# Hybrid decoder layer: a head pair's key-query products issued as one bunch, the second half into another PSUM tag

## The chip, the cores and the metric

The kernel runs on one NeuronCore of a Trainium2 chip. The metric is the device time of one execution in microseconds (us). Five engines take part: TensorE (PE, matmuls; its weight loads are shown apart as PEld), VectorE (DVE), ScalarE (ACT), GpSimd (POOL) and the DMA queues, most of which SyncE (SP) feeds. Results of matmuls land in PSUM, which has eight banks of 128 x 512 float32; DVE and ACT read them out.

## The reference

One decoder layer over 512 tokens of width 1024. Its first half normalises x, projects it, feeds two mixers (an RWKV-7 recurrence of 16 heads of 64 and a sparse attention), merges them by gates and projects back; its second half is a gated MLP with a short causal convolution. The change touches the recurrence only:

```python
def step(state, inp):                       # for each of the 512 tokens, each of the 16 heads
    r_t, w_t, k_t, v_t, a_t, b_t = inp
    sa = jnp.einsum('bhvk,bhk->bhv', state, a_t)
    state = (state * w_t[:, :, None, :] + sa[..., None] * b_t[:, :, None, :]
             + v_t[..., None] * k_t[:, :, None, :])
    return state, jnp.einsum('bhvk,bhk->bhv', state, r_t)
```

## The kernel before

The recurrence isn't run token by token. The 512 tokens are cut into 8 chunks of 64. Inside a chunk everything is matrix products; between chunks a state of 64 x 64 per head is carried on. Heads are worked in pairs p = 0 to 7, one head on partitions 0 to 63 and the other on 64 to 127, and the pairs in two groups of four (g = 0 and 1).

What a pair goes through:

- `inputs(p)` projects the normalised x to K, R and V, three blocks of 8 x 3 matmuls of 128x512 each (lines 297, 298, 299: weight-high times x-high, weight-high times x-low, weight-low times x-high). These are long, and they are what PE does while other work is being prepared.
- `decay(p)` and `prep(p)` make the decay factors and scaled operands. `decay` multiplies `pw` (lines 516, 517) and `pa` (523, 524) into PSUM; ACT turns them into T and A, POOL and DVE go on to EC and EN. `prep` ends with the operands KB (keys and the b vectors, scaled) and AR (a and r, scaled). Line 579 on POOL is the last write of KB.
- `couple(p)` forms, for each chunk c and head h, the 128x128 product of KB and AR: the key-query products, tile `g`, line 607. Chunks 0 to 3 are the half q = 0 and chunks 4 to 7 the half q = 1; a half fills two banks, `g{p}{q}0` and `g{p}{q}1`, one for each head. DVE multiplies each bank with the causal mask into the tile GS in SBUF (line 610) and so frees it. After both halves POOL scales KB for the state (line 617, which overwrites KB and so has to wait until the products have read it), V is transposed into `pv`, a correction is multiplied into `pbo` (626, 627), and the local products `pl` (636) and the transposes `pt` of KB are made.

After a group's four pairs, `invert` inverts the small triangular systems on DVE, and `recur` walks over the 8 chunks (tiles xw, xs, y; `YT` on ACT, line 739, reads `y` out). `stats` and `finish` normalise the result (tiles `gst`, `YT`; lines 787 to 799). They run among the pairs of the second group.

PSUM is shared by four tags of two banks each: `pj` for the projections, `px`, `py` and `pz`. Before the change both halves of `g` use `pz`, as do `pw`, `pa` and `pbo`. `py` holds `pl`, one of the two `pt`, and in the recurrence `y`.

Generators interleave these pieces: `drive` steps the projection of the next pair and, at given rates, `couple`, `decay` and `prep`. Each `yield` is a step. Tile's scheduler then sets each engine's final order by its own list scheduling from that program order, the dependencies and the buffers, so that an edit in `couple` can move instructions of other pieces, on every engine. In the profile a float32 matmul counts twice (x16 for the 8 products of a half), and each product has a weight load of its own, on 64 rows of the array where the projections use 128.

Of the kernel before, what the change touches and what calls it, by code (L numbers as in the profile page):

```python
# [48 lines left out]
def hybrid_layer(ctx: ExitStack, tc: tile.TileContext, a, out, dbg=None, stop=None):  # L49
# [14 lines left out]
    def pj(name):  # L64
        return ps.tile([128, 512], F32, tag="pj", name=name, bufs=2)

    def px(name):
        return ps.tile([128, 512], F32, tag="px", name=name, bufs=2)

    def py(name):  # L70
        return ps.tile([128, 512], F32, tag="py", name=name, bufs=2)

    def pz(name):
        return ps.tile([128, 512], F32, tag="pz", name=name, bufs=2)
# [44 lines left out]
    def tr(o, i, ident):  # L119
        return te.transpose(o, i, ident)  # L120
# [467 lines left out]
    def decayed(p, o, gr):  # L588
        po.tensor_tensor(gr.AR[p % GP][:, 1, :].rearrange(c8, t=64), o.R.rearrange(c8, t=64), o.EC[:, :, 1:65],
                         op=OP.mult)  # L590
        sc.activation(gr.Dc[:, p % GP], o.EC[:, :, 64], AF.Copy)

    def couple(p, o, gr, i):
        V, EC, KB = o.V, o.EC, o.KB
        AR = gr.AR[i]
        if i == 0:
            sc.activation(AR[:, 0, :], o.AR, AF.Copy)
            decayed(p, o, gr)
            yield
        m4 = mask.rearrange("p (s t) -> p s t", t=64)[:, None].to_broadcast([128, 4, 2, 64])  # L600
        for q in range(2):
            gh = [pz(f"g{p}{q}{h}") for h in range(2)]
            for j in range(4):
                c = 4 * q + j
                for h in range(2):
                    hs = slice(h * 64, (h + 1) * 64)
                    te.matmul(gh[h][:, j * 128:(j + 1) * 128], KB[hs, c].rearrange("p s t -> p (s t)"),  # L607
                              AR[hs, :, c * 64:(c + 1) * 64], start=True, stop=True)
            for h in range(2):
                ve.tensor_tensor(gr.GS[:, 0:2 + i:1 + i, 4 * q:4 * q + 4, h].rearrange("p s c t -> p c s t"),  # L610
                                 gh[h].rearrange("p (c s t) -> p c s t", s=2, t=64), m4, op=OP.mult)
            yield
        for b in range(2):
            bs = slice(b * 32, (b + 1) * 32)
            sy.dma_start(gr.ld[b, i].rearrange("c h i t -> i (c h) t"), gr.GS[bs, 0, :, :, bs])
        sy.dma_start(gr.l2[i].rearrange("c h i t -> i (c h) t"), gr.GS[0:32, 0, :, :, 32:64])
        po.tensor_tensor(KB.rearrange("p c s t -> p c (s t)"), KB.rearrange("p c s t -> p c (s t)"),  # L617
                         EC[:, :, 64:65].to_broadcast([128, 8, 128]), op=OP.mult)
        pv = px(f"pv{p}")
        for t in range(4):  # L620
            tr(pv[:, t * 128:t * 128 + 128], V[:, t * 128:t * 128 + 128], ident)
        for q in range(2):
            sc.activation(gr.UV[64:128, q::2, i], pv[64 * q:64 * q + 64].rearrange("p (c h f) -> p c h f", h=2, f=64),
                          AF.Copy)
        pbo = pz(f"pbo{p}")
        te.matmul(pbo, onesr, o.rbh, start=True, stop=False)
        te.matmul(pbo, onesr, o.rbl, start=False, stop=True)
        bv = rw.tile([128, S], F32, tag="T", name=f"bv{p}", bufs=NT)
        ve.tensor_tensor(bv, pbo, V, op=OP.mult)
        yield  # L630
        yield
        sy.dma_start(bvd[p], bv)
        pl = py(f"pl{p}")
        for c in range(8):
            for h in range(2):
                te.matmul(pl[h * 64:(h + 1) * 64, c * 64:(c + 1) * 64], gr.GS[64:128, 0, c, h, :],
                          gr.UV[64:128, c, i, h, :], start=True, stop=True)
        pt = [f(f"pt{p}{q}") for q, f in enumerate((py, px))]
        for c in range(8):
            tr(pt[c // 4][:, c % 4 * 128:c % 4 * 128 + 128], KB[:, c].rearrange("p s t -> p (s t)"), ident)  # L640
        sc.activation(gr.LV[:, i], pl.rearrange(c8, t=64), AF.Copy)
        for q in range(2):
            sc.activation(gr.BKT[i][:, 4 * q:4 * q + 4, :], pt[q].rearrange("p (c f) -> p c f", f=128), AF.Copy)
        yield
# [220 lines left out]
    for g in range(2):  # L865
        group_tiles(g)
        for i in range(GP):
            p = GP * g + i
            if i < GP - 1:
                drive(inputs(p + 1, os_[p + 1]), spawn(couple(p, os_[p], G[g], i), 0, PR),  # L870
                      spawn(later(decay, p + 1, os_[p + 1], pz), 4, 0.5),
                      spawn(later(prep, p + 1, os_[p + 1], pz, G[g]), KD, PK))
            else:
                drive(itertools.chain(*gates_(1)), spawn(couple(p, os_[p], G[g], i), 0, PL))
        if g == 0:
            r0 = core(0)
            fill = itertools.chain(*gates_(NG0), inputs(GP, os_[GP]))
            drive(fill, *r0, spawn(later(decay, GP, os_[GP], pz), 8 * NG0 + 4, 0.5),
                  spawn(later(prep, GP, os_[GP], pz), 8 * (NG0 + 3) + 1, PA))
            f0 = spawn(finish(G[0], 0), 0, FR)  # L880
# [493 lines left out]
    with pool("ff") as ff:  # L1374
# [29 lines left out]
        for j in range(22):  # L1404
            us = []
            for x in range(2):
                blk = 2 * j + x
                if blk < NU:
                    p = pu4[blk]
                    half_up(blk, 1)  # L1410
                else:
                    wh, wl = split_w(a["up"][blk], f"up{blk}")
                    p = pj(f"pu{blk}")
# [242 lines left out]
```

## Time and profile before

| | |
|---|---|
| median of 3 runs | 1181.39 us (1176.57, 1181.39, 1184.37) |
| the profiled execution's own time | 1176.54 us |
| its span | 1174.8 us |
| PE busy, PE weight loads busy | 1144.2 us (97%), 914.0 us (78%) |
| DVE, ACT, POOL busy | 685.8, 604.4, 560.1 us |
| mean granted TensorE clock | 0.992 |
| pairs 0 to 3, products of `g` | 93 to 169 us |
| pairs 4 to 7, products of `g` | 294 to 379 us |

A profile is of one execution, so what is read from it is compared with that execution's time, 1176.54 us, not with the median. In rows of the chain and of the timeline the first number is the start, the second the duration, in us from the span's start. "[0.56 <-DVE GS L610]" at a row's end means that the engine was idle for 0.56 us before it, and that DVE's instruction of line 610 on tile GS ended the wait.

### The profile page before, as it was taken

The page shows a single profiled execution, that of the slowest core. Times are in us where ns is not written, and L with a number is a line of the kernel's source. Part 1 is how long each engine was busy: PE and PEld are TensorE (multiplying, and loading weights), DVE is VectorE, ACT ScalarE, POOL GpSimd, SP SyncE. Part 2 cuts the span into 40 slices and gives each one's busy share as a digit, 9 for nine tenths or more (in the row PEclk, how much of TensorE's full clock was granted, in tenths as well). Part 3 has the DMA queues.
Part 4 walks back from the last instruction along what each step waited for, and adds up shares of the span by engine and source line. Part 5 has one row for each costly group of instructions (what it writes and reads, how often), then busy time and mean ns, then how long its engine had stood idle before and what let it go on. Part 6 is the DMA issues. An engine that isn't in the chain of part 4 may idle for free.

```text
span 1174.8 us, 19913 instructions
## 1 busy us (share of the span) xinstructions
PE 1144.2 (97%) x7316; PEld 914.0 (78%) x7316; DVE 685.8 (58%) x1350; ACT 604.4 (51%) x1208; POOL 560.1 (48%) x535
## 2 busy tenths in 40 slices
PE   8999999999899999999999999999999999999997
PEld 6887788877687888766766777788888888887886
DVE  4245547344655652577699985655443544548776
ACT  5546554433565433476576664443344444446664
POOL 4356765544777553455433212531266666664300
PEclk9999999989999999999999999999999999999999
DMA  6522334530134556236342125551155555559941
GB/s 215 138 74 83 103 111 143 182 89 25 54 105 123 178 161 164 86 99 212 108 126 82 37 64 169 198 200 38 56 143 150 143 146 144 145 152 208 200 112 71
DMA packets 115250, 147.93 MB, mean 126 GB/s; under 512 B 47249, under 2 KB 50129, under 8 KB 114898
## 3 DMA queue, kind: packets, MB, share of 16 engines
q1 hardware_dynamic: 93890, 121.76, 34.1%
q0 software_dynamic: 6336, 11.54, 5.9%
q10 hardware_dynamic: 14928, 13.37, 3.4%
q8 instruction: 57, 0.93, 0.3%
q14 instruction: 39, 0.32, 0.1%
HBM read 124.29 MB, written 21.23 MB: 124 GB/s over the span
## 4 chain that ended last, share of the span: by engine, by line
PE 81%; DVE 7%; issue 5%; POOL 4%; ACT 2%; DMA 1%; SPq 0%; DVEq 0%; POOLq 0%; ACTq 0%
PE pu L193 6%; PE pu L192 6%; PE pu L194 6%; PE da L1465 5%; PE pt L120 3%; PE o L1118 3%; PE db L1465 3%; PE gt L297 2%; PE gt L299 2%; PE gt L298 2%; PE ub L1147 2%; PE ub L1145 2%; PE g L607 2%; PE ub L1146 2%; PE v L297 1%
## 5 line engine op out<-in xcount | busy, mean ns | idle before, releaser
L1420 DVE SCALAR_TENSOR_TENSOR u<-pu,cvec,u 128x511 f32<-128x511 f32 x44 | 32.9, 748 | 98.7 <-ACT u L1419 98.7
L1426 POOL TENSOR_TENSOR ar<-u,u 128x512 f32<-128x512 f32 x22 | 28.7, 1303 | 38.7 <-DVE u L1421 38.7
L658 DVE TENSOR_TENSOR TM<-XL 128x30 f32<-128x30 f32 (+14 forms) x60 | 32.1, 536 | 20.7 <-ACT XL L653 18.7
L1391 ACT ACTIVATE oh<-ar 128x512 fp32r<-128x512 f32 (+1 forms) x44 | 25.1, 573 | 33.9 <-DVE ar L1428 26.6
L1118 PE MATMUL o<-PT,vt 128*64 128x128 f32 (+3 forms) x256 | 40.4, 441 | 0.0
L660 DVE TENSOR_TENSOR XL<-XL,TM 128x30 f32<-128x30 f32 (+14 forms) x60 | 35.7, 596 | 2.2
L1104 ACT ACTIVATE PT<-pt 128x384 f32<-128x384 f32 (+1 forms) x48 | 24.8, 517 | 23.1 <-PE pt L120 22.9
L1419 ACT ACTIVATE u<-pu,cvec 128x512 f32<-128x512 f32 x44 | 33.5, 762 | 5.2 <-PE pu L1355 5.2
L1106 DVE COPY PT<-pt 128x384 f32<-128x384 f32 (+1 forms) x48 | 28.6, 596 | 11.2 <-PE pt L120 10.8
L1421 DVE SCALAR_TENSOR_TENSOR u<-pu,cvec,u 128x510 f32<-128x510 f32 x44 | 32.9, 749 | 1.5
L1392 DVE TENSOR_TENSOR ol<-ar,oh 128x512 fp32r<-128x512 f32 (+1 forms) x44 | 27.1, 620 | 9.0 <-ACT oh L1391 8.8
L521 DVE TENSOR_TENSOR_SCAN C<-rmask,T 128x512 f32<-128x512 f32 x8 | 10.8, 1356 | 36.1 <-POOL T L520 36.0
L610 DVE TENSOR_TENSOR GS<-g,mask 128x512 f32<-128x512 f32 x32 | 20.7, 685 | 14.3 <-PE g L607 14.3
L1118 PEld LDWEIGHTS o<-PT,vt 128*64 128x64 f32 x256 | 15.6, 136 | 14.9 <-issue 11.7
L607 PEld LDWEIGHTS g<-AR,KB 64*128 64x128 f32 x256 | 18.9, 192 | 8.9 <-DVE GS L610 3.9
L607 PE MATMUL g<-AR,KB 64*128 64x128 f32 x256 | 22.3, 291 | 2.9 <-POOL KB L579 1.4
L1428 DVE TENSOR_TENSOR ar<-ar 128x256 f32<-128x256 f32 x11 | 15.4, 1398 | 15.8 <-POOL ar L1426 15.8
L1423 ACT ACTIVATE u<-u 128x512 f32<-128x512 f32 x22 | 13.7, 624 | 18.8 <-DVE u L1421 18.7
L977 POOL TENSOR_SCALAR rh<-dist 128x512 f32<-128x512 f32 x16 | 10.3, 643 | 26.0 <-DVE stt L1023 13.2
L766 ACT ACTIVATE UV<-xs 64x256 f32<-64x256 f32 x16 | 6.1, 379 | 31.6 <-PE xs L671 23.2
L617 POOL TENSOR_TENSOR KB<-KB,EC 128x1024 f32<-128x1024 f32 x8 | 15.3, 1917 | 11.5 <-PE g L607 6.2
L1321 PE MATMUL wo<-woh,mh 128*128 128x512 f32 x52 | 20.4, 392 | 0.0
(2710 smaller groups left out, 4324.6 us busy)
## 6 DMA issues: line engine op xcount, KB each, us to landing
wt<-in_down_dram POOLq DMA_DIRECT2D x33, 256.0 KB, 5.0
gtd<-gt ACTq DMA_DIRECT2D x16, 256.0 KB, 2.0
qs<-qd SPq DMA_DIRECT2D x32, 128.0 KB, 2.9
g<-gtd SPq DMA_DIRECT2D x16, 256.0 KB, 3.4
wt<-in_down_dram SPq DMA_DIRECT2D x11, 256.0 KB, 3.2
w<-in_down_dram SPq DMA_DIRECT2D x11, 256.0 KB, 3.3
w<-in_down_dram POOLq DMA_DIRECT2D x11, 256.0 KB, 4.7
dna<-in_down_dram SPq DMA_DIRECT2D x11, 256.0 KB, 4.7
```

The costliest lines, as they stand in the source:

```text
L120: return te.transpose(o, i, ident)
L192: te.matmul(p, wh(k), mh(k), start=first and k == 0, stop=False)
L193: te.matmul(p, wh(k), ml(k), start=False, stop=False)
L194: te.matmul(p, wl(k), mh(k), start=False, stop=last and k == n - 1)
L297: te.matmul(p, wh(k), hh[:, k, :], start=k == 0, stop=False)
L607: te.matmul(gh[h][:, j * 128:(j + 1) * 128], KB[hs, c].rearrange("p s t -> p (s t)"), AR[hs, :, c * 64:(c + 1) * 64], start=True, stop=True)
L660: ve.tensor_tensor(XU[:, j + 1:32, 0:j], XU[:, j + 1:32, 0:j], tm, op=OP.add)
L1118: te.matmul(po8[e * 64:e * 64 + 64, j * 128:], vt[:, j, b * 256 + g * 64:b * 256 + g * 64 + 64], PT[j, e], start=False, stop=b == 1 and j ...
L1419: sc.activation(u, p, AF.Identity, scale=cvec[:, cv + 2:cv + 3], bias=cvec[:, cv + 3:cv + 4])
L1420: ve.scalar_tensor_tensor(u[:, 1:], p[:, :S - 1], cvec[:, cv + 1:cv + 2], u[:, 1:], op0=OP.mult, op1=OP.add)
L1421: ve.scalar_tensor_tensor(u[:, 2:], p[:, :S - 2], cvec[:, cv:cv + 1], u[:, 2:], op0=OP.mult, op1=OP.add)
L1465: te.matmul(acc[m], l[k][:, x, tsl], w[r], start=first and i == 0, stop=last and i == 2, skip_group_check=True)
```

## The change

Both halves' products are issued one after the other as one bunch of 16, ahead of either half's masking. The first half still takes `pz`, the second takes `py`.

```diff
@@ couple
+        gq = []
         for q in range(2):
-            gh = [pz(f"g{p}{q}{h}") for h in range(2)]
+            gh = [(pz, py)[q](f"g{p}{q}{h}") for h in range(2)]
             for j in range(4):
                 c = 4 * q + j
                 for h in range(2):
                     hs = slice(h * 64, (h + 1) * 64)
                     te.matmul(gh[h][:, j * 128:(j + 1) * 128], KB[hs, c].rearrange("p s t -> p (s t)"),
                               AR[hs, :, c * 64:(c + 1) * 64], start=True, stop=True)
+            gq.append(gh)
+        for q, gh in enumerate(gq):
             for h in range(2):
                 ve.tensor_tensor(gr.GS[:, 0:2 + i:1 + i, 4 * q:4 * q + 4, h].rearrange("p s c t -> p c s t"),
                                  gh[h].rearrange("p (c s t) -> p c s t", s=2, t=64), m4, op=OP.mult)
             yield
```

The lines behind it stand three further down (607 becomes 608, 610 becomes 613, 617 becomes 620). The number of instructions stays the same. On TensorE the scheduler moves other rows at two of the eight pairs, 0 and 4; at the others the products alone move. On ScalarE rows move at the same two pairs, on GpSimd at 0, 4 and 6, on VectorE at 4, and on SP some loads and stores change places near pairs 4 and 6.

TensorE at pair 0, from the end of the first half on, before (the digits of `g` are pair, half, head; `k1` is the next pair's projection, `pv0` a transpose of V):

```order
L607 MATMUL g000_963<-AR00_916,KB0_857 128x128
L607 MATMUL g001_964<-AR00_916,KB0_857 128x128
L298 MATMUL k1_938<-hl_110,w7h1_945 128x512
L299 MATMUL k1_938<-hh_109,w7l1_946 128x512
L297 MATMUL k1_938<-hh_109,w7h1_945 128x512
L607 MATMUL g010_981<-AR00_916,KB0_857 128x128 x3
L607 MATMUL g011_982<-AR00_916,KB0_857 128x128 x3
L607 MATMUL g010_981<-AR00_916,KB0_857 128x128
L607 MATMUL g011_982<-AR00_916,KB0_857 128x128
L298 MATMUL k1_938<-hl_110,w7h1_945 128x512
L299 MATMUL k1_938<-hh_109,w7l1_946 128x512
L120 MATMUL pv0_1016<-ident_81,V0_824 128x128 x2
```

The same place now:

```order
L608 MATMUL g010_973<-AR00_916,KB0_857 128x128
L608 MATMUL g011_974<-AR00_916,KB0_857 128x128
L298 MATMUL k1_938<-hl_110,w7h1_945 128x512
L299 MATMUL k1_938<-hh_109,w7l1_946 128x512
L516 MATMUL pw1_993<-ltw_398,lh1_931 128x512
L517 MATMUL pw1_993<-ltw_398,ll1_932 128x512
L523 MATMUL pa1_1001<-lta_399,lh1_931 128x512
L524 MATMUL pa1_1001<-lta_399,ll1_932 128x512
```

The eight products of the second half follow the first half's eight directly (these rows begin with the last two of them), and `pw` and `pa` of the next pair come ahead of `pv0`. At pairs 1, 2, 3, 5, 6 and 7 the bunch closes in the same way, and the three to seven rows that stood between the halves now stand behind it.

TensorE at pair 4, where the first group's recurrence ends, before (from behind the first half on; `r5` is the next pair's projection, `pt40` and `pt41` the transposes of KB):

```order
L120 MATMUL pv4_3111<-ident_81,V4_2539 128x128 x4
L299 MATMUL r5_3132<-hh_109,w18l0_3134 128x512
L297 MATMUL r5_3132<-hh_109,w18h1_3139 128x512
L298 MATMUL r5_3132<-hl_110,w18h1_3139 128x512
L607 MATMUL g410_3073<-AR10_3004,KB4_2661 128x128 x4
L607 MATMUL g411_3074<-AR10_3004,KB4_2661 128x128 x4
L636 MATMUL pl4_3161<-UV1_3013,GS1_3008 64x64 x2
L516 MATMUL pw5_3085<-ltw_398,lh5_3019 128x512
L517 MATMUL pw5_3085<-ltw_398,ll5_3020 128x512
L636 MATMUL pl4_3161<-UV1_3013,GS1_3008 64x64 x7
L120 MATMUL pt40_3178<-ident_81,KB4_2661 128x128 x3
L523 MATMUL pa5_3093<-lta_399,lh5_3019 128x512
```

The same place now, from the last two products on:

```order
L608 MATMUL g410_3065<-AR10_3004,KB4_2661 128x128
L608 MATMUL g411_3066<-AR10_3004,KB4_2661 128x128
L516 MATMUL pw5_3085<-ltw_398,lh5_3019 128x512
L517 MATMUL pw5_3085<-ltw_398,ll5_3020 128x512
L523 MATMUL pa5_3093<-lta_399,lh5_3019 128x512
L524 MATMUL pa5_3093<-lta_399,ll5_3020 128x512
L120 MATMUL pv4_3111<-ident_81,V4_2539 128x128 x4
L120 MATMUL pt41_3179<-ident_81,KB4_2661 128x128 x4
L299 MATMUL r5_3132<-hh_109,w18l0_3134 128x512
L297 MATMUL r5_3132<-hh_109,w18h1_3139 128x512
L298 MATMUL r5_3132<-hl_110,w18h1_3139 128x512
L299 MATMUL r5_3132<-hh_109,w18l1_3140 128x512
```

Here `pw5`, `pa5`, `pv4` and half of the transposes of KB moved to just behind the bunch, ahead of the projection rows that stood between the halves, and the local products `pl4` moved behind those.

GpSimd at the same place, before (`w20l1` is a weight's low part for V of pair 5, `YT0` the recurrence's output, `T5` and `F5` are decay factors of pair 5):

```order
L508 MEMSET TT1_3015 32x32x32 x2
L140 TENSOR_TENSOR w20l1_3244<-w201r_3245,w20h1_3243 128x512
L789 TENSOR_TENSOR YT0_2528<-YT0_2528,gst01_3051 128x512
L617 TENSOR_TENSOR KB4_2661<-KB4_2661,EC4_2354 128x1024
L534 MEMSET EC6_3452 128x8
L789 TENSOR_TENSOR YT0_2528<-YT0_2528,gst01_3051 128x512
L520 TENSOR_SCALAR T5_3089<-T5_3089 128x512
L528 TENSOR_SCALAR F5_3098<-A5_3096,vd_94 128x512
```

And now:

```order
L508 MEMSET TT1_3015 32x32x32 x2
L792 TENSOR_TENSOR YT0_2528<-YT0_2528,gst01_3051 128x512
L620 TENSOR_TENSOR KB4_2661<-KB4_2661,EC4_2354 128x1024
L534 MEMSET EC6_3452 128x8
L140 TENSOR_TENSOR w20l1_3244<-w201r_3245,w20h1_3243 128x512
L520 TENSOR_SCALAR T5_3089<-T5_3089 128x512
L792 TENSOR_TENSOR YT0_2528<-YT0_2528,gst01_3051 128x512
L528 TENSOR_SCALAR F5_3098<-A5_3096,vd_94 128x512
```

The weight's low part moved behind the scaling of KB, and the second `YT0` behind `T5`. On VectorE the four maskings of pair 4 stand closer together, the third and fourth ahead of two reductions of `stats`.

## The prediction

> **What bounds the kernel now.** I read the page first, its busy shares and its costliest groups. The columns of a group are the count, busy us and mean ns of one, and behind the second bar the engine's idle time just before them with what ended most of it.
>
> ```profile
> PE 1144.2 (97%) x7316; PEld 914.0 (78%) x7316; DVE 685.8 (58%) x1350; ACT 604.4 (51%) x1208; POOL 560.1 (48%) x535
> ...
> L610 DVE TENSOR_TENSOR GS<-g,mask 128x512 f32<-128x512 f32 x32 | 20.7, 685 | 14.3 <-PE g L607 14.3
> ...
> L607 PEld LDWEIGHTS g<-AR,KB 64*128 64x128 f32 x256 | 18.9, 192 | 8.9 <-DVE GS L610 3.9
> L607 PE MATMUL g<-AR,KB 64*128 64x128 f32 x256 | 22.3, 291 | 2.9 <-POOL KB L579 1.4
> ```
>
> TensorE is the bound: busy for 97% of the span, so only what shortens its own stream, or a wait in it, moves the end. The products of `g` are 22.3 us of that stream, about 1.9%. They had 8.9 us of idle weight loading ahead of them, of which 3.9 us were ended by the maskings of line 610. The change can't remove any of the 22.3 us. It can remove waits for a masking, and whatever it costs TensorE to turn from the projections to the products and back twice instead of once. So the stake is a few us of 1176.5, and the question is how many.
>
> The second view is the chain of waits around a pair where nothing waits, pair 1, from its second half on (start, duration, what):
>
> ```profile
> 118.48 1.09 PE g L607 x16
> 119.57 0.43 PE k L297
> 120.00 0.23 PE k L298
> ```
>
> A projection matmul takes 0.23 us here, but the first one behind a half takes 0.43 us. Each half so costs 1.09 us plus 0.20 us of turning. How long eight more products last inside a running bunch I take from their weight loads at pair 7, with which they are paced:
>
> ```profile
> 374.50 0.97 PEld L607 LDWEIGHTS g<-AR,KB 64*128 64x128 f32 x16 [0.35 <-POOL w60l L140]
> ```
>
> 16 loads in 0.97 us. A second half that follows the first directly should thus add 0.97 us, and the projection that stood behind it falls back to 0.23 us.
>
> **The change, pair by pair.** It adds and removes no instruction. At each pair I set what the second half and the projection behind it take now against 0.97 + 0.23 = 1.20 us.
>
> *Pairs 1, 2 and 6, where no masking is waited for.* Pair 1 is above; the second halves of pairs 2 and 6 are
>
> ```profile
> 143.14 1.09 PE g L607 x16
> 350.41 1.09 PE g L607 x16
> ```
>
> so each has 1.09 + 0.43 = 1.52 us and saves 0.32 us: **0.96 us** for the three. Bounds for one pair: 0.20 us, if the bunch runs no tighter than two halves, and 0.55 us, the whole of 0.12 + 0.43. I take 0.32, since both its parts are rows.
>
> *Pairs 0 and 3, where the second half is stretched.* Both halves want the two banks of `pz`, and with only three projection rows between them the masking hasn't freed the second bank when the first is refilled:
>
> ```profile
> 95.06 1.64 PE g L607 x16
> 96.70 0.43 PE k L298
> ...
> 166.93 1.63 PE g L607 x15
> 168.56 0.43 PE gt L297
> ```
>
> 1.64 + 0.43 and 1.63 + 0.43 become 1.20 each: 0.87 and 0.86, together **1.73 us**. The second half has banks of its own in `py`, whose last users there, `pl` and `pt` of the pair before, were read out long ago. At pair 0 `pw` and `pa` now come two projections behind the bunch and want the `pz` banks; the maskings start as the first half ends, take 0.69 us each and run beside the second half's 0.97 us, so I cost that at nothing.
>
> *Pair 7, the longest wait.* Here DVE comes late to the maskings, so the second half first waits and is then stretched. The first row is of the timeline, the second of the chain:
>
> ```profile
> 377.34 1.75 PE L607 MATMUL g<-AR,KB 64*128 64x128 f32 x16 [0.79 <-DVE GS L610]
> 379.10 0.43 PE gt L297
> ```
>
> 0.79 + 1.75 + 0.43 = 2.97 us become 1.20: **1.77 us**, the largest term. What is late next is the masking itself, which no longer holds up TensorE, since the local products that read GS stand well behind it in its order.
>
> *Pair 5, at a lowered clock.* The first row is of the timeline, the next of the chain; the last is of the view by stretches, which has columns of busy us per engine, then the granted clock, the DMA share and GB/s:
>
> ```profile
> 317.99 0.50 PE L299 MATMUL k<-hh,w22l 128*128 128x512 f32 x1 [2.75 <-POOL w22l L140]
> 322.23 0.43 PE k L298
> ...
> 323.08 1.51 PE g L607 x16
> 324.59 0.43 PE k L297
> 319.00:325.00 6.00, 5.79 (x40) 4.48 (x41) 1.67 (x3) 0.63 (x1) 3.92 (x6) 0.72 0.54 167
> ```
>
> TensorE waits 2.75 us for a weight's low part from POOL, and then runs at a mean clock of 0.72: a projection takes 0.43 us, the second half 1.51. The saving lies between the 0.32 of a quiet pair and 1.51 + 0.43 - 0.97 - 0.43 = 0.54, if the bunch runs before the clock falls. I take **0.4 us**.
>
> *Pair 4, where the order changes.* This is the one place where a masking wait may only change its name (the timeline, engine by engine):
>
> ```profile
> 295.19 1.08 ACT L739 ACTIVATE YT<-y 128x512 f32<-128x512 f32 x2 [0.85 <-PE y L671]
> 297.29 1.26 POOL L140 TENSOR_TENSOR w20l<-w201r,w20h 128x512 fp32r<-128x512 f32 x1 [1.31 <-PE r L299]
> 297.64 0.96 PEld L607 LDWEIGHTS g<-AR,KB 64*128 64x128 f32 x8 [0.56 <-DVE GS L610]
> 298.50 0.68 DVE L610 TENSOR_TENSOR GS<-g,mask 128x512 f32<-128x512 f32 x1
> 298.73 1.04 POOL L789 TENSOR_TENSOR YT<-YT,gst 128x512 f32<-128x512 f32 x1 [0.17 <-DVE gst L788]
> 299.23 0.96 PEld L607 LDWEIGHTS g<-AR,KB 64*128 64x128 f32 x8 [0.62 <-DVE GS L610]
> 300.47 1.91 POOL L617 TENSOR_TENSOR KB<-KB,EC 128x1024 f32<-128x1024 f32 x1 [0.70 <-PE g L607]
> 301.75 0.69 ACT L519 ACTIVATE T<-pw,vd 128x512 f32<-128x512 f32 x1
> 302.44 0.55 PE L120 MATMUL pt<-ident,KB 128*128 128x128 f32 x3 [0.52 <-POOL KB L617]
> 304.98 0.48 PE L299 MATMUL r<-hh,w18l 128*128 128x512 f32 x1
> ```
>
> Two waits of 0.56 and 0.62 us for maskings go. New ones come. The second half takes the `py` banks, which hold the recurrence's last `y` until ACT has read it at 296.27, about when the first half ends: some 0.1 us. `pa` wants the bank that the second masking frees at 299.2. And four transposes of KB now stand ahead of four projections and wait for line 617 on POOL; that is behind `YT`, ends no sooner than 298.73 + 1.04 + 1.91 = 301.7, and finds TensorE ready at about 300.1 (`pa` and `pv` behind 299.2, some 0.9 us): 1.6 us. Walking the new order on (transposes 0.5, four projections 1.1, `pbo` 0.5 behind `T` at 302.4, `pl` and the other transposes some 1.7), I come to the fifth projection at about 305.4. Before, the fourth starts at 304.98 and the fifth 0.3 us later: the same. So **0**, with ends at +1.2 us (the two waits go and nothing takes their place) and -1.6 us (the wait for KB comes on top).
>
> What the maskings would cost if they set the pace: four of 0.69 us are 2.8 us against a bunch of 2.1 us, 0.7 us for each pair. In the rows of pair 1 they run beside projections, and only pair 4 puts users of those banks straight behind the bunch, so I charge nothing here and keep it as a rival.
> The Trainium skill, "TensorEngine Tiling (Array Packing)", "PSUM Bottleneck", speaks against the change: packing speeds up TensorE but not the reading out of PSUM, which may become the limit. By it the sum would be that rival's; the stretched halves of pairs 0 and 3 agree with it, the rows of pair 1 don't.
>
> The same place sets pair 5's wait of 2.75 us, through POOL's chain to the weight's low part. There `w20l`, 1.3 us, now stands ahead of T and the second `YT`, while `pa`, from which A and F follow, comes sooner. These pull against each other; I take 0, with the 1.3 us of `w20l` as the end on either side. On SP a load for the first group's output moves behind two weight loads at pair 6; no product waits for it.
>
> **The sum**: 0.96 + 1.73 + 1.77 + 0.4 + 0 = 4.9 us. The profiled execution, 1176.54 us, of which the span is 1174.8, would become 1171.6. But 1176.54 is the lowest of the four executions known (with 1176.57, 1181.39 and 1184.37); their median is 1179.0, and the median of the three runs 1181.39. A new median will probably not sit on the lowest edge either, so I put the forecast at 1179.0 - 4.9 = **1174 us**.
>
> **Rivals.** That the change isn't made can be left out: the order shows one bunch at all eight pairs.
>
> *The cold stretch at pair 5 goes too.* If the wait of 2.75 us shrinks, the clock may not fall. The stretch costs six projections x 0.20 us and 1.51 - 1.09 on the half: about 1.6 us. With half of the 1.2 us from pair 4: 4.9 + 0.6 + 1.6 = 7.1 us, so 1172 (1169.4 on the profile's basis). For it, among the eight pairs the clock falls behind this wait alone, the longest there, so it may hang on its length. Against it, POOL's order is not clearly better.
> The Trainium skill, "TensorE: Matmul & The Clock Gate", "Part 1: The HAM clock gate (the "warmup" mystery)", says that the clock is halved after about 3.4 us of idling and released after as long a busy stretch. By that rule a wait cut by half a us would more likely leave the clock up; projections of 0.43 against 0.23 us agree with a halved clock.
>
> *The maskings set the pace.* 0.7 us on each pair, as above, 5.6 us in all: 1179.0 - 4.9 + 5.6 = 1180, no change. For it, TensorE's 3.9 us behind maskings; against it, that those waits are for the same two banks, and the second half no longer uses them.
>
> *The gain is given back.* At pairs 4 to 7 TensorE also waits for POOL (2.75 us above), and if POOL sets the pace, what pairs 4 to 7 save, 2.2 us, is waited for at the next weight; pairs 0 and 3 may lose part to later waits. 1.5 to 2.5 us remain: 1177. Against it, behind pair 7 hardly anything is left that waits:
>
> ```profile
> 384.00:500.00 116.00, 114.89 (x1103) 93.13 (x1099) 59.08 (x129) 47.41 (x89) 53.63 (x53) 0.99 0.50 146
> ```
>
> TensorE is busy there for 114.89 of 116 us, so time won at pair 7 should stay won.
>
> *Slower: the longer bunch trips the clock.* The bunch uses 64 of 128 rows for 2.1 us on end. If the throttle takes that for idling, each pair pays a slow stretch like pair 5's, 1.6 us. On the seven others that is 11.2 - 4.9 = 6.3 us lost, so 1185; it decides from the fourth pair on (3 x 1.6 = 4.8). Against it:
>
> ```profile
> 102.06 1.08 PE pl L636 x32
> 103.14 1.03 PE pt L120 x8
> 102.00:126.00 24.00, 24.00 (x190) 19.52 (x191) 12.95 (x20) 15.58 (x28) 17.83 (x16) 1.00 0.41 113
> ```
>
> 2.1 us of still smaller products and transposes in a row left the clock at 1.00.
>
> **How the numbers follow.** Forecast 0.55, cold stretch gone 0.15, given back 0.15, maskings 0.05, slower 0.1. The executions known already differ by 7.8 us, more than the gain. The low end is the cold-stretch case on the profile's basis with the good ends of pairs 4 and 5, 1176.5 - 4.9 - 1.2 - 1.3 - 1.6 = 1167.5, a little lower for the quiet pairs' 0.55: 1166. The high end is 2 us of gain on the highest run, 1184.4 - 2 = 1182.4, so 1183; it leaves out the slow case and little else. About 1% (12 us) is what a measurement of this kernel can tell from no change, and the whole forecast lies inside it. Faster by more than that needs nearly every good end together, or a low draw: 0.12. Slower needs the clock case on all pairs and a high draw: 0.06. Within it 0.82.
>
> **What would show it.** In the new profile: one bunch of 32 rows per pair, about 2.1 us, with one projection of 0.43 us behind it; no wait of line 608 for a masking; at pair 7 the bunch ending near 376.6 less what was won before; at pair 4 a new wait of `pt` for KB of 1 to 2 us; granted clock 1.00 around pairs 0 to 3. I would be wrong if pair 4 or 5 loses more than 2 us, or if the clock falls where it was 1.00.

## The result, and the profile after

The changed kernel takes 1171.99 us (median of six runs, 1171.11 to 1175.05) where the kernel before takes 1179.81 us (six runs, 1176.57 to 1184.37): a ratio of 0.995 with a 95% interval of 0.9929 to 0.997 (the ratios here are the record's, taken over all executions; the quotient of these two medians, 0.9934, lies inside the interval). Timed a second time, it stands at 0.997 (0.9954 to 0.9985). The profiled execution takes 1171.48 us (span 1169.7) against 1176.54 (1174.8).

The page of the changed kernel, its busy shares and the group of the maskings (columns as before):

```profile
PE 1140.1 (97%) x7316; PEld 912.6 (78%) x7316; DVE 686.7 (59%) x1350; ACT 605.0 (52%) x1208; POOL 562.3 (48%) x535
...
L613 DVE TENSOR_TENSOR GS<-g,mask 128x512 f32<-128x512 f32 x32 | 19.9, 683 | 2.0 <-PE g L608 2.0
```

TensorE's busy time went down by 4.1 us, although it does the same instructions. What ended the idle time ahead of the products, from the view of line 608 (us, times):

```profile
  POOL KB L579: 5.1, 7
  POOL AR L589: 0.5, 2
  issue: 0.4, 1
```

No masking is among them any more. Pair 1 in the timeline of the kernel before, from the projection ahead of its second half on:

```profile
118.08 0.40 PE L299 MATMUL k<-hh,w10l 128*128 128x512 f32 x1
118.41 1.16 PE L607 MATMUL g<-AR,KB 64*128 64x128 f32 x16
119.50 0.50 PE L297 MATMUL k<-hh,w10h 128*128 128x512 f32 x1
119.84 0.39 PE L298 MATMUL k<-hl,w10h 128*128 128x512 f32 x1
```

The products at pair 1 and at pair 7 of the changed kernel, each with the row behind it:

```profile
114.87 2.06 PE L608 MATMUL g<-AR,KB 64*128 64x128 f32 x32
116.85 0.50 PE L297 MATMUL k<-hh,w10h 128*128 128x512 f32 x1
117.19 0.39 PE L298 MATMUL k<-hl,w10h 128*128 128x512 f32 x1
...
369.10 2.06 PE L608 MATMUL g<-AR,KB 64*128 64x128 f32 x32
371.08 0.50 PE L297 MATMUL gt<-hh,w60h 128*128 128x512 f32 x1
```

A bunch takes 1.98 us from its first row to the next projection, and that one takes 0.34 us to the next. Before, each half took 1.09 us to the next projection, that one again 0.34, and the projection ahead of the second half 0.33, where projections in a row start 0.23 apart. So TensorE turns from projections to products and back once instead of twice. Where TensorE waits between 88 and 400 us (us in total, times, longest):

```profile
PE pn L557 <- ACT Q L543: 1.8, 1, 1.8
PE g L608 <- POOL KB L579: 1.6, 2, 1.0
PE pt L120 <- POOL KB L620: 1.3, 1, 1.3
...
PE pw L516 <- DVE GS L613: 0.2, 1, 0.2
```

The first is new, the third was 0.52 us, the last is the only one for a masking; the 2.75 us at pair 5 for `w22l`, the low part of the weight for the next pair's K, are gone.

The starts of the same rows in the two timelines show where the time was won. A row's last column is what was won since the row above:

| row on TensorE | before, us | after, us | shift | won since the row above |
|---|---|---|---|---|
| first product of pair 0 | 93.00 | 93.12 | +0.12 | |
| pair 1 | 115.72 | 114.87 | -0.85 | 0.97 (pair 0) |
| pair 2 | 140.38 | 139.09 | -1.29 | 0.44 (pair 1) |
| pair 3 | 164.87 | 163.13 | -1.74 | 0.45 (pair 2) |
| local products of pair 3 | 173.02 | 170.35 | -2.67 | 0.93 (pair 3) |
| pair 4 | 294.05 | 291.21 | -2.84 | 0.17 |
| pair 5 | 319.21 | 316.24 | -2.97 | 0.13 (pair 4) |
| pair 6 | 347.22 | 342.25 | -4.97 | 2.00 (pair 5) |
| pair 7 | 374.50 | 369.10 | -5.40 | 0.43 (pair 6) |
| local products of pair 7 | 383.56 | 376.32 | -7.24 | 1.84 (pair 7) |
| first transpose of the causal products | 510.44 | 504.39 | -6.05 | -1.19 |
| output projection | 772.54 | 766.99 | -5.55 | -0.50 |
| last matmul's end | 1168.13 | 1163.06 | -5.07 | -0.48 |

So 7.36 us are won by the end of the pairs, and 2.2 us are lost again behind them.

### The profile page after: what moved, and what is told of

It is laid out like the page before. It is cut to its first block, busy times and chain, and to the rows that moved or that the text cites. A ratio compares the mean times of both kernels' runs of the same rounds, so it can differ in the third digit from the quotient of the medians.

```text
span 1169.7 us, 19917 instructions
## 1 busy us (share of the span) xinstructions
PE 1140.1 (97%) x7316; PEld 912.6 (78%) x7316; DVE 686.7 (59%) x1350; ACT 605.0 (52%) x1208; POOL 562.3 (48%) x535
## 4 chain that ended last, share of the span: by engine, by line
PE 80%; DVE 8%; issue 4%; POOL 3%; ACT 3%; DMA 2%; SPq 0%; DVEq 0%; POOLq 0%; ACTq 0%
PE pu L192 6%; PE pu L193 6%; PE pu L194 6%; PE da L1468 5%; PE pt L120 3%; PE o L1121 3%; PE db L1468 3%; PE gt L297 3%; PE gt L299 2%; PE gt L298 2%; PE ub L1150 2%; PE v L297 2%; PE ub L1148 2%; PE v L299 2%; PE ub L1149 2%
## 5 line engine op out<-in xcount | busy, mean ns | idle before, releaser
L663 DVE TENSOR_TENSOR XL<-XL,TM 128x30 f32<-128x30 f32 (+14 forms) x60 | 43.2, 720 | 2.2
L661 DVE TENSOR_TENSOR TM<-XL 128x30 f32<-128x30 f32 (+14 forms) x60 | 25.2, 420 | 20.7 <-ACT XL L656 18.7
L980 POOL TENSOR_SCALAR rh<-dist 128x512 f32<-128x512 f32 x16 | 10.3, 645 | 24.7 <-DVE stt L1026 13.1
L1326 PE MATMUL wo<-woh,ml 128*128 128x512 f32 x52 | 20.3, 390 | 0.0
L1325 PE MATMUL wo<-wol,mh 128*128 128x512 f32 x52 | 20.3, 390 | 0.0
L579 POOL TENSOR_TENSOR KB<-KB,EN 128x512 f32<-128x512 f32 x8 | 13.3, 1667 | 14.4 <-DVE rb L577 14.4
```

The lines of the kernel that those rows point to most:

```text
L663: ve.tensor_tensor(XU[:, j + 1:32, 0:j], XU[:, j + 1:32, 0:j], tm, op=OP.add)
```

## The experiments

The first question is which half of the change brings the time, the tag or the bunch? The theory was that both do, each its part; the rivals are in the expectations. What a kernel wins or loses at a pair is read as in the table, from the starts of the same rows.

### The tag alone

The halves are masked one after the other as before; the second half has banks of its own.

```diff
-            gh = [pz(f"g{p}{q}{h}") for h in range(2)]
+            gh = [(pz, py)[q](f"g{p}{q}{h}") for h in range(2)]
```

> Two halves as before, each masked before the next is issued, but the second half in py. If the gain is the sum of two separate parts (waits for the banks of pz, and turning TensorE twice per pair), the waits alone go: pairs 0, 3 and 7 save about 0.55 + 0.54 + 1.45 us = 2.5 us, the quiet pairs nothing, and a projection behind each of the two halves still takes 0.43 us: ratio 0.998. Rival, the gain comes from the order at pairs 4 and 5 that the tag brings with it: then this run has about 2 us more of it (the same order stands there), ratio 0.996. Rival, the bunch is what counts: ratio 1.000.

Measured: 1175.2 us, ratio 0.9975 (0.9956 to 0.9994), span 1172.4. The second half of pair 0 in the timeline of the kernel before, then those of pairs 0 and 7 with the tag alone:

```profile
94.99 1.71 PE L607 MATMUL g<-AR,KB 64*128 64x128 f32 x16
```

```profile
94.67 1.16 PE L607 MATMUL g<-AR,KB 64*128 64x128 f32 x16
...
374.31 1.16 PE L607 MATMUL g<-AR,KB 64*128 64x128 f32 x16
```

The stretch (1.71 and 1.75 us before) and the 0.79 us of waiting are gone with the tag alone; pairs 0, 3 and 7 win 0.55, 0.54 and 1.45 us, the quiet pairs 0.02 us or less either way. From pair 4 to pair 6 it wins 1.68 us, so the rival of the order holds beside the theory; the interval of the ratio holds both numbers, 0.998 and 0.996. The turning stays: of the 7.36 us the tag brings 3.54 by the end of the pairs, and some 0.6 us more were lost in this execution to a slow stretch of the clock, between pairs 3 and 4, that is 3.41 us longer here.

### The bunch alone

The source gives the products as one bunch, but both halves keep `pz`.

```diff
-            gh = [(pz, py)[q](f"g{p}{q}{h}") for h in range(2)]
+            gh = [pz(f"g{p}{q}{h}") for h in range(2)]
```

> Both halves traced ahead of the maskings, but both in pz. TensorE can't close the bunch, since the second half needs the banks that the first half's maskings free; the order now has three projections between the halves at pairs 1, 2, 5 and 6 where six stood. If waits for banks count, pairs 1, 2 and 6 are now stretched like pairs 0 and 3, by 0.5 us each, and nothing is saved: ratio 1.001 to 1.002. If bunching by itself brought the gain: 0.998 or below.

Measured: 1185.37 us, ratio 1.0051 (1.0035 to 1.0067): slower, and by more than expected. Pair 1's second half:

```profile
118.11 1.70 PE L608 MATMUL g<-AR,KB 64*128 64x128 f32 x16
```

With both halves in two banks the scheduler does not form a bunch on TensorE. It puts the second half three projections behind the first instead of six, so that at the quiet pairs too it is refilled as the banks come free: 1.70 instead of 1.16 us, 0.49 to 0.54 us lost at pairs 1, 2 and 6. Pair 5 loses 1.79 us in a slow stretch of the clock that is twice as long as before. This profile is of the fastest of the twelve executions. The mean granted clock of the twelve is 0.985, in the profiled one 0.990 and in the kernel before, timed beside them, 0.9905: part of the ratio is slow clock that this profile doesn't show. The bunch brings time only with the tag.

### The change without pair 4, and at pair 4 alone

Pair 4 is where the order of other rows moves. In the first kernel that pair is as before, in the second it alone is changed. The edit is against the kernel before; `products` is the old loop over the matmuls, made a function.

```diff
-        for q in range(2):
-            gh = [pz(f"g{p}{q}{h}") for h in range(2)]
+        def products(q, tag):
+            gh = [tag(f"g{p}{q}{h}") for h in range(2)]
...
+            return gh
+
+        bunch = p != 4          # the other kernel: p == 4
+        gq = [products(0, pz), products(1, py)] if bunch else []
+        for q in range(2):
+            gh = gq[q] if bunch else products(q, (pz, pz)[q])
```

> The change at seven pairs; pair 4 keeps its two halves in pz and its old order on every engine. The sum of the prediction without pair 4 (which was 0) gives -4.9 us, ratio 0.996, with TensorE's wait of 2.75 us for w22l at pair 5 and the slow stretch behind it still there. Rival, read from the profile after: the new order at pair 4 moves the slow stretch away from pair 5's products and is worth about 1.7 us; then this run stands 1.7 us behind the full change, -3.4 us, ratio 0.997. In the profile: pair 4's start to pair 6's start 53.2 us as before, against 51.1 with the full change.

> The change at pair 4 alone, the other seven pairs as before; there the second half's tag brings the products 8 projections' and a transposition's length forward. Theory (pair 4's reorder is worth little: the waits it takes away at pairs 4 and 5 come back as the waits for the key scaling and the norm): profile 0 to -1.0 us at pair 6's products against before, ratio 0.999 to 1.000. Rival (the reorder pays through pair 5, as the difference of the two profiles with and without it says: -1.3 us from pair 3's last step to pair 6, -1.6 at the end): ratio 0.9985.

Measured: 0.9968 (0.9953 to 0.9982), 1174.26 us, and 0.9999 (0.9989 to 1.001), 1177.67 us. From the first product of pair 4 to that of pair 6 the kernel before takes 53.17 us. The first kernel wins 1.99 us of it, where the expectation had nothing, the second 1.65, the whole change 2.13: the two are no sum, since the kernel without pair 4 had no slow stretch of the clock there and the others had one. At pair 4 alone the profile's 1.65 us can't be seen in the medians. The waits from 288 to 345 us and the clock from 290 to 340 us, of the kernel without pair 4:

```profile
PE k L299 <- POOL w22l L140: 2.8, 1, 2.8
...
290.00:340.00 50.00, 44.77 (x360) 35.45 (x360) 30.36 (x44) 31.95 (x56) 39.12 (x37) 1.00 0.28 76
```

This is of use for the clock: the wait of 2.8 us is there as in the kernel before, and the clock stayed at 1.00 behind it.

### The change at pair 7 alone

The same edit with `p == 7`.

> The change at pair 7 alone, where the largest single term stands. Predicted: TensorE stands 1.77 us earlier behind pair 7 (local products pl at 381.8 instead of 383.56 us), ratio 0.9985 if that stays won to the end. Rival, that what is won before the attention is given back there (the profile after shows 7.2 us won at this place and 5.1 at the end): 0.5 us or less at the end, ratio 1.000, with the loss between 450 and 720 us. Third, that the later drift is only the difference of two executions: then the profile shows any shift of up to 2 us behind 450 us, of either sign.

Measured: 1178.75 us, ratio 1.000 (0.9985 to 1.0014). In its profile pair 7 wins 1.84 us, as in the whole change:

```profile
377.68 2.06 PE L607 MATMUL g<-AR,KB 64*128 64x128 f32 x32
...
463.00:518.00 55.00, 53.33 (x819) 41.46 (x816) 31.70 (x96) 24.36 (x62) 23.50 (x33) 0.91 0.29 90
```

However, 2.7 us are lost in the second group's recurrence, where the mean clock is 0.91 against 0.97 before. Whether the medians keep the 1.84 us stays open: the interval holds both ends of the expectation, and the profiled execution is the slowest of the twelve.

### Every product twice

```diff
-                    te.matmul(gh[h][:, j * 128:(j + 1) * 128], ...)
+                    for _ in range(2):
+                        te.matmul(gh[h][:, j * 128:(j + 1) * 128], ...)
```

> The changed kernel with every key-query product given twice in a row, so the half-array bunch lasts 4.1 us instead of 2.06 at each of the eight pairs; the output stays the same. Theory (a bunch costs its own products and nothing else): +2.0 us per pair, 8 x 2.0 = 16.0 us on the changed kernel's 1171.5 in its profiled execution, 1187.5 us, ratio to the kernel before about 1.009; TensorE's granted clock stays 1.00 at pairs 0 to 3 and the projections behind each bunch keep 0.24 us apart. Rival (a longer half-array stretch costs clock): a slowed stretch of up to 1.6 us per pair on top, 8 x 1.6 = 12.8 us more, 1200 us, ratio 1.02, with projections 0.43 us apart behind the bunches.

Measured: 1188.13 us, ratio 1.009 (1.0056 to 1.0125), the number of the theory. Pair 1 and the clock around pairs 0 to 3 and 4 to 7:

```profile
115.89 3.94 PE L609 MATMUL g<-AR,KB 64*128 64x128 f32 x64
...
93.00:175.00 82.00, 82.00 (x656) 68.70 (x655) 45.08 (x58) 45.57 (x78) 56.15 (x47) 1.00 0.30 86
290.00:390.00 100.00, 95.12 (x876) 77.74 (x877) 54.00 (x76) 54.95 (x96) 73.41 (x65) 1.00 0.31 89
```

Even 3.94 us on half the rows leave the clock at 1.00 in this execution. It is the fastest of four; two of the others take 8 and 10 us more, at a mean clock of 0.986 and 0.985 against 0.990, and for those no profile shows where the clock fell. Pairs 0 to 3 each cost 1.88 to 1.93 us more than in the changed kernel; at pairs 4 and 5 together only 1.7 us come on top for two bunches, since part goes into waits that are there anyway, and the clock has no slow stretch there in this execution.

### Pair 5's GpSimd steps moved to VectorE

In the changed kernel TensorE waits at pair 5 for Q, which comes from T: the rows are of POOL, DVE and PE in the timeline of the changed kernel.

```profile
297.97 0.66 PE L120 MATMUL pt<-ident,KB 128*128 128x128 f32 x4 [1.33 <-POOL KB L620]
298.94 1.28 POOL L140 TENSOR_TENSOR w20l<-w201r,w20h 128x512 fp32r<-128x512 f32 x1 [0.85 <-PE r L299]
300.31 0.62 POOL L520 TENSOR_SCALAR T<-T 128x512 f32<-128x512 f32 x1
300.97 2.05 DVE L521 TENSOR_TENSOR_SCAN C<-rmask,T 128x512 f32<-128x512 f32 x1 [2.74 <-POOL T L520]
306.33 1.18 PE L557 MATMUL pn<-sel,Q 128*128 128x2 f32 x8 [1.81 <-ACT Q L543]
316.24 2.06 PE L608 MATMUL g<-AR,KB 64*128 64x128 f32 x32 [0.97 <-POOL KB L579]
```

The first kernel moves T to VectorE, the second also the last write of KB (line 579) and the decayed receptance (AR, line 589), by the same edit.

```diff
-        po.tensor_scalar(T, T, -0.5 * KAPPA, ...)
+        (ve if p == 5 else po).tensor_scalar(T, T, -0.5 * KAPPA, ...)
```

> The changed kernel with one step moved: the scaling of pair 5's decay logits (T, 128x512) goes to VectorE, which stands idle 2.74 us for it, instead of GpSimd, where the weight split w20l stands ahead of it. Theory (the chain T, scan, exponentials, Q holds TensorE 1.81 us at pair 5's norms and starts the slowed stretch of projections behind it): T ends about 0.9 us earlier, so the wait falls from 1.81 to 0.5 to 0.9 us; with the slowed stretch of 7 projections (0.43 us apart instead of 0.24, 1.3 us) gone too, -2.2 us, without it -0.9 to -1.3 us; about 1169 to 1170.5 in the profile, ratio to before 0.993 to 0.994. Rival (the wait only moves on, to the key scaling of line 579 ahead of pair 5's products, 0.97 us in the changed kernel): no change, ratio 0.995.

> f3_decay_scale_vector with two more of pair 5's steps on VectorE instead of GpSimd: the key scaling (KB, line 579) and the decayed receptance (AR, line 589), while VectorE waits 2.94 us for the products there. Theory (pair 5 waits for GpSimd's queue and for nothing else: in the run before, 2.31 us for w22l and 0.72 for KB): the weight split w22l comes 1.65 us earlier, KB lies ahead of the products, the two waits shrink to about 0.5 us together, so pair 5's products start 2.0 to 2.5 us earlier after pair 4's; against f3's profile (span 1167.2) about -2 us, ratio to before 0.9935 to 0.9945. Rival (something behind GpSimd, the weights' DMA or VectorE's own queue, comes just as late): less than 0.7 us at pair 5, ratio 0.9955.

Measured: 0.9956 (0.9938 to 0.9973), 1172.47 us, and 0.9952 (0.9939 to 0.9966), 1173.11 us. TensorE's waits from 288 to 345 us, first of the kernel that moves T (with its clock from 290 to 340 us below), then of the other:

```profile
PE k L299 <- POOL w22l L140: 2.3, 1, 2.3
...
PE pn L557 <- ACT Q L543: 0.2, 1, 0.2
...
290.00:340.00 50.00, 44.98 (x322) 35.14 (x322) 31.15 (x43) 32.22 (x56) 41.36 (x37) 1.00 0.30 85
```

```profile
PE g L608 <- DVE AR L589: 1.1, 1, 1.1
PE k L299 <- POOL w22l L140: 0.7, 1, 0.7
```

The wait for Q went from 1.8 to 0.2 us as the theory had it, and `w22l`'s came back with 2.3: the rival was right in kind, though it named another row. From pair 4 to pair 6 it wins 0.66 us more than the change. In the second kernel `w22l` comes 1.56 us earlier after pair 4's products, nearly as the theory had it, and its wait falls to 0.7 us; but 1.1 us are now waited for AR, in VectorE's queue. Pair 5's products start 23.92 us after pair 4's where it was 24.38: 0.46 us earlier, not 2.0 to 2.5, so by its own measure the rival was right (less than 0.7, something comes just as late). Up to pair 6 it wins 1.13 us more than the first. Neither can be told from the changed kernel by its time (0.995 and 0.997), so no version here is shown to beat it.

### Both kernels once more

The two kernels without any edit, each for a second profile (their lines stand one further down).

> The changed kernel itself once more, for a second profile. If the 1.2 us lost at the recurrence's first local solves behind pair 7 (slow windows of the clock, 2 instead of 1 in the kernel before) belong to the change, this profile loses them again at the same place, 2 us of won time by the start of the output projection instead of pair 7's 7.2. If slow windows fall where they happen to fall, the won time at pair 7's last step is again 7.0 to 7.4 us and what is left of it further on differs by 1 us or more from the first profile. Ratio 0.993 to 0.997 either way.

> The kernel before once more, for a second profile. If the 1.1 us that the changed kernel loses at the recurrence's first local solves behind pair 7 belongs to the change, this profile shows the clock's mean of 0.97 in that stretch again (461 to 516 us) and the same gaps; the profiles of the two then differ there by 1.0 to 1.2 us as before. If the slow windows fall where they happen to fall, this profile may show 0.94 there, and up to 1.2 us more between the last pair and the causal products than the first profile of before. Ratio 1.000 within 0.002.

Measured: 0.997 (0.9954 to 0.9985) and 1.0002 (0.9988 to 1.0016). The second group's recurrence, first in the second profile of the changed kernel, then in that of the kernel before (the column behind POOL's is the clock):

```profile
455.00:510.00 55.00, 52.41 (x811) 40.22 (x808) 32.41 (x98) 25.17 (x64) 25.36 (x35) 0.94 0.33 101
```

```profile
462.00:517.00 55.00, 52.50 (x828) 39.92 (x826) 32.31 (x97) 25.09 (x64) 25.17 (x35) 0.97 0.32 99
```

Against the first profile of the kernel before, the changed kernel again wins 7.28 us over the pairs and again loses 1.1 us there, at a mean clock of 0.94 in both of its profiles, where the kernel before has 0.97 in both. In these four profiles the loss goes with the kernel. Over all twelve it doesn't: the changed kernel with every product twice has one slow window of the clock there, as the kernel before, and the kernels changed at pair 4 alone and at pair 7 alone have two and three. The timed executions point a little to the change: beside the second profile the mean granted clock was 0.989 in the changed kernel (seven executions) and 0.991 in the kernel before (22). So it stays open how much of the loss belongs to the change; the last section has what the profiles show of it.

## Why the prediction was right, point by point

The forecast was 1174 us, and the measured median is 1172, the ratio 0.995 to 0.997. The sum was 4.9 us on the profile's basis; the two profiled spans differ by 5.1. That they agree so well is partly luck: 7.4 us were won and 2.2 lost, and the prediction had neither number. Its mechanism held at all pairs but 4 and 5.

- **Quiet pairs**, 0.32 us each: 0.44, 0.45 and 0.43. The mechanism is as told; the term was too small by 0.12 us. By the starts of the rows the second half adds 0.89 us to the bunch (1.98 less 1.09) and not the 0.97 of the weight loads, so 0.20 us come from the products. The turning that goes is 0.10 us into the second half (0.33 less 0.23) and 0.11 out of it (0.34 less 0.23); the sum had 0.20 for the second of these and nothing for the first.
- **Pairs 0 and 3**, 0.87 and 0.86: 0.97 and 0.93. The tag alone brings 0.55 and 0.54 of it (the stretch), the bunch the rest (the turning). `pw` and `pa` behind the bunch wait at no place but pair 4, and there 0.2 us.
- **Pair 7**, 1.77: 1.84 and, at pair 7 alone, 1.84.
- **Pair 5**, 0.4: with the change 0.45 us more from pair 4 to pair 6 than with the tag alone (2.13 against 1.68), where everything else is in the same order. The number fits for another reason than was given: the 0.4 was worked out for products at a lowered clock, but the slow stretch now lies ahead of them, and at 1.00 this is a quiet pair's 0.44.
- **Pair 4**, 0, is the step that failed, together with the waits at pair 5, which were taken as unchanged. With the tag alone, which makes the same order, the stretch from pair 4 to pair 6 is 1.68 us shorter. The halves at pair 4, in the timeline of the kernel before and then of the changed one:

```profile
295.30 0.93 PE L607 MATMUL g<-AR,KB 64*128 64x128 f32 x10
...
297.64 1.16 PE L607 MATMUL g<-AR,KB 64*128 64x128 f32 x8
299.23 1.16 PE L607 MATMUL g<-AR,KB 64*128 64x128 f32 x8 [0.43 <-DVE GS L610]
300.31 0.33 PE L636 MATMUL pl<-UV,GS 64*64 64x64 f32 x4
```

```profile
292.46 2.18 PE L608 MATMUL g<-AR,KB 64*128 64x128 f32 x26
294.80 0.50 PE L516 MATMUL pw<-ltw,lh 128*128 128x512 f32 x1 [0.16 <-DVE GS L613]
```

The old second half takes 2.67 us, from 297.64 to 300.31. Now the first half's last ten rows and the second half together take 2.34 us to `pw`; the ten took 0.87 us before (to the transposes of V at 296.17), so the second half adds 1.47 us, more than the 0.97 of the sum. That saves 1.20 us. The new wait for KB was foreseen at 1.6 us and measured 1.33, but a wait of 0.52 for the same row went, so it costs 0.81: pair 4 itself wins 0.4. Pair 5's 2.75 us for `w22l` became 1.81 for Q, and the wait for line 579 grew from 0.73 to 0.97: 0.7 won. Together this is 1.1 of the 1.68 us; the other 0.6 lie among the rows that changed places and are not assigned. Both parts stay within the ends that the prediction gave (1.2 and 1.3 us). All this is read from profiles; in the medians the kernel changed at pair 4 alone shows no gain (0.9999).

- **The rivals.** The maskings set no pace: they sit idle for the products for 2.0 us where it was 14.3, and nothing but 0.2 us of TensorE's time waits for them. By that, the Trainium skill's rule ("TensorEngine Tiling (Array Packing)", "PSUM Bottleneck") does not decide here. The longer bunch doesn't trip the clock: in no profile does a slow stretch begin within 10 us behind a bunch, not even at twice the length. The gain of pairs 6 and 7 isn't given back to GpSimd (0.43 and 1.84 us won); the rival's 2.2 us, by the way, leave out pair 6: 0.4 + 0.32 + 1.77 is 2.5. The cold stretch at pair 5 did not go. It moved ahead of the products, with the same 0.57 in these two stretches (before, then after):

```profile
320.00:324.00 4.00, 4.00 (x24) 2.85 (x22) 1.29 (x2) 0.63 (x1) 2.63 (x4) 0.57 0.47 142
```

```profile
307.00:311.00 4.00, 4.00 (x14) 3.24 (x14) 3.51 (x7) 3.57 (x8) 2.08 (x3) 0.57 0.01 4
```

That is why the table shows 2.00 us at pair 5 and 0.13 at pair 4: only the sum of the two says something. The guess that the stretch hangs on the length of the wait is wrong: it came behind 2.75 us in the kernel before, behind 1.81 in the changed one, and not behind 2.8 without pair 4 nor behind 2.31 with T moved.

- **"Time won at pair 7 should stay won"** was argued from a row with TensorE busy for 114.89 of 116 us. It stayed won for 70 us. A busy engine can still lose time, by its clock: 1.2 us there, and 1.0 us (2.5 in the second profile) further on. Of the latter, 0.6 us are waits: behind the first transposes of the causal products TensorE's waits add up to 9.2 us in the kernel before and 9.8 in the changed one (9.4 and 10.3 in the second profiles). The largest part is one wait for the second half's normalised input (`n2p` for `n2xn`), 1.4 us in both profiles of the kernel before and 1.6 in both of the changed one. The rest I can't assign.

## What to carry to other kernels

When a second batch of small products waits for the reading out of the first, give it PSUM banks of its own first, and then close the batches up: here the banks brought about half of the gain, closing up the other half, and closing up without the banks cost 0.5%. Where a change lets the scheduler reorder several engines, look for the wait that takes the place of the one removed: at pair 5 it went from `w22l` (2.75 us) to Q (1.81) and back to `w22l` (2.31). Below 2 us in 1172, one profile of each kernel doesn't decide; a second profile of the same kernels showed that the 7.3 us over the pairs repeat, and the profiles of the other kernels that the loss behind them need not.

## What was not expected of the hardware

**The slow stretches of the clock lie on a grid.** Read in pieces of half a us, the granted clock in these executions is 1.00 or 0.50, apart from pieces in which it changes. From 90 us on to the end of the causal products every slow stretch is 3.41, 6.83 or 10.24 us long, and inside one execution the starts of all of them differ by multiples of 3.413 us to within 0.05: 252.24, 320.50 and 467.28 in the kernel before (20 and 43 steps), 249.09, 307.12 and 457.30 in the changed one (17 and 44). The phase differs between executions. The second group's recurrence, first of the kernel before, then of the changed one (with a row of its timeline):

```profile
464.00:467.00 3.00, 2.75 (x66) 2.37 (x62) 1.69 (x3) 0.18 (x1) 0.00 (x0) 1.00 0.72 226
467.00:470.00 3.00, 2.75 (x27) 2.20 (x27) 0.42 (x1) 1.35 (x3) 2.21 (x3) 0.55 0.23 82
```

```profile
453.00:457.00 4.00, 4.00 (x98) 3.52 (x97) 1.32 (x2) 0.00 (x0) 0.00 (x0) 1.00 0.46 147
...
454.13 2.14 PE L674 MATMUL mt<-x 32*32 32x32 f32 x62
...
457.00:464.00 7.00, 6.53 (x85) 5.42 (x81) 1.87 (x4) 1.42 (x3) 2.39 (x3) 0.52 0.34 104
```

In the twelve profiles this place has one slow window when a line of the grid falls 0.1 to 0.5 us after the start of the group's first 32x32 products (442.45 us in the changed kernel; counted modulo 3.413 us; four executions), and two or three when it falls 1.1 to 3.1 us after (eight). So what a kernel wins ahead of such a place can cost it a window there, some 1.1 us. Whether a wait of 1.8 to 2.8 us is followed by a slow window may hang on the grid too, but that is not shown. Some of the spread of one kernel's runs goes with the clock: in the 83 timed executions of the kernel before for which both are on record, time and mean clock have a correlation of -0.41. The link to the grid is read from twelve executions and not tested by an edit: nothing here moves the grid by itself.

The Trainium skill, "TensorE: Matmul & The Clock Gate", "Part 1: The HAM clock gate (the "warmup" mystery)", gives this gate a free-running window of 3413 ns and only two rates, the full and the half. The rows agree with both. By the Trainium skill the rate is set by how busy TensorE has been. The row of 453 us shows that this isn't the busy time of the profile: TensorE is busy for all of 4.00 us, from 454.13 on with products of 32x32, and the next window, from 457.30 on, is slow.

**A VectorE step can stand behind a GpSimd step.** An elementwise product of the same size on VectorE shows it in the changed kernel: line 545 takes 0.69 us at 236.87 us, where GpSimd does nothing, and 1.78 us at 354.91, where it begins 0.07 us behind a split of line 140 on GpSimd. From the timeline of the kernel with all three steps moved:

```profile
311.03 1.27 DVE L579 TENSOR_TENSOR KB<-KB,EN 128x512 f32<-128x512 f32 x1
312.22 1.76 DVE L589 TENSOR_TENSOR AR<-R,EC 128x512 f32<-128x512 f32 x1
...
310.48 1.27 POOL L140 TENSOR_TENSOR w22l<-w220r,w22h 128x512 fp32r<-128x512 f32 x1
311.71 1.72 POOL L140 TENSOR_TENSOR w22l<-w221r,w22h 128x512 fp32r<-128x512 f32 x1
```

Each of the two VectorE steps ends 0.55 us after the GpSimd row that was running when it began (311.75 and 313.43), as line 545's does at 354.91. GpSimd pays as well: of the 240 splits of this size in the changed kernel, the 48 with no VectorE row beside them take 1.26 to 1.30 us, and 26 take 1.5 or more, all with VectorE rows beside them. At 0.69 us each, the two steps would have ended at 312.4 (an estimate from these rows), ahead of TensorE, which waited for AR from 313.02 on. A step that is moved off a late queue to an idle engine can stand behind the same queue there.
